# Value projection as seven block products ahead of the heads, and the heads' steps in two queues

## The chip, the cores and the metric

One core of one Trainium2 chip runs the whole layer in one launch. The metric is device time in microseconds, the median of three runs.

## The reference, cut to what matters

One encoder layer on 512 tokens of width 2048, in float32: a token mixer of 8 differential-attention heads and 8 stick-breaking heads, cross-attention into 256 memory tokens, and a SwiGLU feed-forward. Each part has an RMS norm before and after it and a residual. What the change touches:

```python
h = rms_norm(x, g_mix_pre[l])
proj = h @ w_in[l]                      # 2048 x 6144: queries, keys, values of both kinds
a_q, a_k, a_v, b_q, b_k, b_v = jnp.split(proj, ...)
...
out_a = diff_attention(a_q, a_k, a_v, ...)   # 8 heads of 128
out_b = stick_breaking(b_q, b_k, b_v, ...)   # 8 heads of 128
mix = jnp.concatenate([out_a, out_b], axis=-1) @ w_out[l]
```

The values `a_v` and `b_v` together are a product of 512x2048 by 2048x2048.

## The kernel before, in words

**Precision.** Every float32 operand is split in two float32r parts, high and low; a product is three matmuls (high by high, high by low, low by high) that add up in PSUM. A matmul has a 128x128 stationary operand and up to 512 moving columns.

**Weights.** Class `Weights` (L75) goes through a fixed list of chunks of 128x1024 floats (512 KB), in the order in which the kernel uses them. A chunk is loaded by SP's queue into one of `NR` = 5 raw slots, split by ScalarE (L122, a cast) and VectorE (L123, a subtraction) into one of three slots of `parts`, and read by TensorE. `get` (L138) splits two chunks ahead of the one it hands out. For the feed-forward a chunk can be an "add": the raw slot of an earlier chunk stays, and POOL's queue adds another block of the weights to it in flight (L131). Three more raw slots are handed out there by `more` (L94).

**Stages.** The memory stage (`mem_ticks`, L503) projects the memory to keys and values: 64 chunks of 16 matmuls. Beside it the generator `setup_gen` (L416) loads x, takes its norm, and writes the normalised, transposed and split x into the tile `big` (L461 to 469): 16 multiplications (L464) and 16 splits (L231, L232). Then come four groups of four heads (L768): `v_block` (L585) projects the values of a group for all 512 tokens, with 8 chunks of 24 matmuls, and keeps them in SBUF; then each head projects its queries and its keys (`ws_proj`, L540: 48 matmuls each). Then `w_out` (L902), the cross-attention, and the feed-forward, whose products are already done by class `Blocks` (L1184): a product of two by two blocks in seven block products instead of eight, with sums of blocks ahead of it and behind it.

**Side work.** What a head does behind its projections (`diff_gen` L643, `sb_gen` L713, `subnorm` L616) is a generator in the queue `side` (class `Side`, L151): one head at a time. Every six matmuls of a projection call `fill` (L319), which lets `side` go one step, once the number that the step before yielded has been counted down: calls if it is whole, microseconds if it is a float. A step issues some matmuls and the ScalarE and VectorE work on their results; the next step's matmuls read that work. The numbers `YI`, `YS`, `YT`, `SY`, `SZ` and `SL` (L60, L61) are these gaps. The results `mixT` wait in a pool of 50 tiles until `big` is free; the first block of `w_out` runs all of `side` that is left before its last chunk (L907).

**Order.** Beyond the program, a scheduler orders the instructions of each engine; where `pin` (L235) is passed, they stay in program order. An engine runs its instructions in order.

Of the kernel before, what the change touches and what calls it, by code (L numbers as in the profile page):

```python
# [11 lines left out]
F32 = mybir.dt.float32  # L12
# [8 lines left out]
P = 128  # L21
D = 2048
S = 512
# [161 lines left out]

@with_exitstack
def encoder_kernel(ctx: ExitStack, tc: tile.TileContext, a: dict, out: bass.AP):
# [96 lines left out]
    gu_cbs = [(j, NFB + j) for j in range(NFB)]  # L284
    dn_c0 = [2 * sum(DOWN[:b]) for b in range(len(DOWN))]
# [7 lines left out]
    col_pairs = [(0, 1), (2, 3)]  # L293
# [121 lines left out]

    def setup_gen():  # L416
# [34 lines left out]
        def load_xT(kt):  # L451
            if kt < KT:
                xT[kt] = u(s="xT")
                dma(xT[kt], a["xT"][kt])

        for kt in range(3):
            load_xT(kt)
# [43 lines left out]
    unscaled, rbm_done = deque(), []  # L501

    def mem_ticks(name, ct, dst):  # L503
# [18 lines left out]
        while rbm_done and unscaled:  # L522
            t, dst = unscaled.popleft()
            nc.vector.tensor_tensor(t[:, M:512], t[:, 0:M], rbm, op=ALU.mult)
            dma(dst, t[:, M:512])
        fill()
# [13 lines left out]
    def ws_proj(name, ct, lo=0, hi=S):  # L540
        p = ps()
        for half in range(2):
            wh, wl = W.get((name, ct, half))
            wh = wh.rearrange("p (a b) -> p a b", a=8)
            wl = wl.rearrange("p (a b) -> p a b", a=8)
            for k in range(8):
                kt = half * 8 + k
                o, xh, xl = p[:, lo:hi], big[:, 0, kt, lo:hi], big[:, 1, kt, lo:hi]
                mm(o, wh[:, k], xh, start=(kt == 0), stop=False)
                mm(o, wh[:, k], xl, start=False, stop=False)  # L550
                mm(o, wl[:, k], xh, start=False, stop=(kt == KT - 1))
                if k % 2 and kt < KT - 1 and (hi - lo == S or k % 4 == 3):
                    fill()
        return p
# [30 lines left out]
    def v_block(g):  # L585
        accs = [ps() for _ in range(NT)]
        for c in range(8):
            tok_ticks("w_v", g, c, range(NT), accs, from_big, VA <= c < VF)
        r = []
        for t in range(NT):  # L590
            h, l = u(F32R, "vh"), u(F32R, "vl")
            split(h, l, accs[t])
            r.append((h, l))
        fill()
# [21 lines left out]
    def subnorm(o, head, g):  # L616
# [7 lines left out]
        yield 2 if head < KT - 1 else 6.0  # L624
# [142 lines left out]

    for g in range(4):  # L768
        v = v_block(g)
        for h in range(4 * g, 4 * g + 4):  # L770
# [410 lines left out]
    def sub2(o, x, y):  # L1181
        return nc.vector.tensor_tensor(o, x, y, op=ALU.subtract)

    class Blocks:  # L1184

        def __init__(self, name, cbs, c0, n, done, base=None, tile=fu, src=None, every=1,
                     need=None):  # L1190
            self.name, self.cbs, self.c0, self.n, self.done = name, cbs, c0, n, done
            self.base, self.tile, self.src, self.every = base, tile, src or ffn_part, every
            self.T, self.m, self.need = {}, 0, need

        def load_base(self, th, nh):
            if self.base:
                for t in range(2):
                    b = self.T["b", 2 * th + t, nh] = self.tile("base")
                    dma(b, self.base(2 * th + t, nh))

        def product(self, i, apart=False):

            quarter = {1: (0, 0), 5: (0, 1), 3: (1, 1), 6: (1, 0)}.get(i)
            if quarter:
                self.load_base(*quarter)
            p = (ps(), ps())
            ws = []
            for c in range(self.n):
                if self.need:
                    self.need(i, c)  # L1210
                ws.append(W.get((self.name, self.cbs, self.c0 + c, i)))
                if apart:
                    continue
                for k in range(2):
                    for t in range(2):
                        self.mms(p[t], i, c, k, t, ws[c])
            while later:
                later.popleft()()
            for t in range(2):
                if apart:  # L1220
                    for c in range(self.n):
                        for k in range(2):
                            self.mms(p[t], i, c, k, t, ws[c])
                self.evict(i, t, p[t])
                if apart:
                    while later:
                        later.popleft()()

        def mms(self, p, i, c, k, t, w):
            kt = 2 * c + k  # L1230
            wh, wl = (x.rearrange("p (a b) -> p a b", a=2)[:, k] for x in w)
            fh, fl = self.src(i, kt, t)
            mm(p, fh, wh, kt == 0, False)
            mm(p, fh, wl, False, False)
            mm(p, fl, wh, False, kt == 2 * self.n - 1)
            self.m += 1
            if self.m % self.every == 0:
                fill(0.68 * self.every)

        def evict(self, i, t, p):  # L1240

            T = self.T
            add = lambda o, x, y: nc.vector.tensor_tensor(o, x, y, op=ALU.add)
            b = lambda t, nh: T.pop(("b", t, nh))
            if i in (1, 5, 3) or i == 7 and ("r", t) not in T:
                T[i, t] = self.tile(f"p{i}_")
                if i == 3 and self.base:
                    add(T[i, t], p, b(t, 1))
                else:
                    nc.scalar.copy(T[i, t], p)  # L1250
            elif i == 2:
                c = T.pop((1, t)) if ("r", t) in T else self.tile("c11_")
                add(c, p, T.get((1, t), c))
                T["c11", t] = c
                if self.base:
                    later.append(lambda: add(c, c, b(t, 0)))
                later.append(lambda: self.done(t, 0, c))
            elif i == 6:
                r = T.pop((1, t)) if ("c11", t) in T else self.tile("r_")
                sub2(r, p, T.get((1, t), r))  # L1260
# [294 lines left out]
```

## Time and profile before

| what | value |
|---|---|
| median of three runs | 2713.6 us (2713.14 to 2714.34) |
| the profiled execution's own time | 2713.2 us |
| its span, first to last instruction | 2711.4 us |
| TensorE busy | 2665.7 us, 98% |
| VectorE, ScalarE, GpSimd busy | 1636.6, 1294.1, 231.3 us |
| mean granted TensorE clock | 0.996 |
| memory stage, first matmul to last | 7.2 to 194.3 us |
| heads, value blocks included | 194.3 to 842 us |
| output projection starts beside the last heads | 842 us |

Busy time of TensorE is a union of spans whose ends are modelled, since matmuls overlap: the 389 ns that the profile gives for one matmul of 512 columns is its latency, and the spacing of a row of them is read from the time line. Idle time of an engine that nobody waits for costs nothing.

### The profile page before, as it was taken

To read this page: it belongs to the slowest core of one execution; us is meant where nothing else is said; L and a number is where in the kernel's file an instruction comes from. 1 tells how busy PE (TensorE), PEld (TensorE's weight loads), DVE (VectorE), ACT (ScalarE), POOL (GpSimd) and SP (SyncE) were. 2 spreads that over 40 slices of the span, in tenths; PEclk is the share of its full clock that TensorE was granted. 3 is DMA by queue.
4 is the path that set the end of the run, shared out by engine and by line. 5 is a ranking of instruction groups with operands and counts; after the bars stand their busy time and mean duration, and the time that the engine had idled before them with its cause. 6 is when DMAs were issued, how large, how long until landed. Compare 5 with 4: busy or idle time off the path is not lost.

```text
span 2711.4 us, 33630 instructions
## 1 busy us (share of the span) xinstructions
PE 2665.7 (98%) x12704; PEld 2212.9 (82%) x12704; DVE 1636.6 (60%) x2260; ACT 1294.1 (48%) x1892; POOL 231.3 (9%) x273
## 2 busy tenths in 40 slices
PE   8999999999999999999999999999999999999996
PEld 7888777778888789988888888888888888878775
DVE  6672555554445357435567665555556568797887
ACT  5542444445556346334456444444444456454453
POOL 0000000000000000000001212211111121111101
PEclk9999999999999999999999999999999999999998
DMA  8873222222222366223557999888898998788776
GB/s 292 295 266 105 82 86 86 82 82 70 82 80 84 102 212 231 74 98 123 161 173 190 245 256 208 200 204 203 204 209 195 209 223 246 203 263 202 201 204 204
DMA packets 163139, 470.15 MB, mean 173 GB/s; under 512 B 18208, under 2 KB 28856, under 8 KB 162976
## 3 DMA queue, kind: packets, MB, share of 16 engines
q1 hardware_dynamic: 128352, 346.47, 37.7%
q0 software_dynamic: 34624, 121.54, 24.2%
q8 instruction: 99, 1.62, 0.3%
q14 instruction: 64, 0.52, 0.1%
HBM read 431.21 MB, written 39.34 MB: 174 GB/s over the span
## 4 chain that ended last, share of the span: by engine, by line
PE 92%; issue 3%; DVE 2%; DMA 2%; ACT 1%; POOL 1%; SPq 0%; POOLq 0%; ACTq 0%; DVEq 0%
PE ps L228 90%; PE ps L1301 1%; DVE parts L123 1%; DMA xnat<-in_x_dram 1%; PE ps L848 1%; DMA raw<-in_w_dn_dram 0%; ACT parts L122 0%; PE ps L700 0%; POOL y_d L1421 0%; DMA xres<-x_d 0%; DMA raws<-in_w_mk_dram 0%; POOL raws L131 0%; PE ps L982 0%; POOL raw L131 0%; DMA raws<-in_w_dn_dram 0%
## 5 line engine op out<-in xcount | busy, mean ns | idle before, releaser
L228 PE MATMUL ps<-parts,big 128*128 128x512 f32 x4992 | 1168.0, 391 | 10.0 <-ACT parts L122 5.3
L228 PEld LDWEIGHTS ps<-parts,big 128*128 128x128 f32 x4992 | 933.3, 188 | 210.2 <-DVE parts L123 8.0
L123 DVE TENSOR_TENSOR parts<-raws,parts 128x1024 fp32r<-128x1024 f32 x548 | 668.8, 1223 | 596.5 <-ACT parts L122 588.0
L122 ACT CAST parts<-raws 128x1024 fp32r<-128x1024 f32 x548 | 576.3, 1053 | 735.9 <-PE ps L228 666.7
L228 PE MATMUL ps<-parts,form 128*128 128x512 f32 x2376 | 552.4, 390 | 2.3 <-ACT parts L122 2.0
L228 PEld LDWEIGHTS ps<-parts,form 128*128 128x128 f32 x2376 | 444.7, 188 | 96.8 <-ACT parts L122 4.2
L228 PE MATMUL ps<-big,parts 128*128 128x512 f32 x1536 | 375.0, 394 | 0.0
L228 PEld LDWEIGHTS ps<-big,parts 128*128 128x128 f32 x1536 | 282.5, 188 | 61.9 <-issue 4.2
L123 DVE TENSOR_TENSOR parts<-raw,parts 128x1024 fp32r<-128x1024 f32 x178 | 217.0, 1222 | 149.6 <-ACT parts L122 146.1
L122 ACT CAST parts<-raw 128x1024 fp32r<-128x1024 f32 x178 | 187.3, 1054 | 195.7 <-PE ps L228 153.2
L228 PE MATMUL ps<-memhl,parts 128*128 128x512 f32 (+1 forms) x1024 | 183.8, 341 | 8.9 <-DVE memhl L239 7.2
L228 PEld LDWEIGHTS ps<-memhl,parts 128*128 128x128 f32 x1024 | 158.1, 190 | 33.9 <-DVE memhl L239 7.6
L131 POOL DMA_DIRECT2D raws<-in_w_gu_dram x108 | 93.6, 867 | 825.6 <-DVE parts L123 633.4
L380 POOL TENSOR_TENSOR small<-small 128x1 f32<-128x1 f32 (+2 forms) x22 | 16.8, 770 | 1018.9 <-DVE small L379 999.9
L228 PE MATMUL ps<-khl,parts 128*128 128x256 f32 x768 | 96.2, 285 | 0.0
L228 PEld LDWEIGHTS ps<-khl,parts 128*128 128x128 f32 x768 | 93.3, 192 | 0.2
L228 PE MATMUL ps<-big,pTh 128*128 128x512 f32 x256 | 80.2, 392 | 0.0
L228 PE MATMUL ps<-gh,big 128*128 128x512 f32 x256 | 79.2, 389 | 0.0
L131 POOL DMA_DIRECT2D raw<-in_w_gu_dram x60 | 51.9, 866 | 114.0 <-DVE parts L123 114.0
L677 ACT ACTIVATE e<-e,small 128x512 f32<-128x512 f32 (+3 forms) x64 | 35.5, 555 | 53.8 <-DVE small L675 53.8
L228 PEld LDWEIGHTS ps<-gh,big 128*128 128x128 f32 x256 | 48.1, 188 | 9.9
L228 PEld LDWEIGHTS ps<-big,pTh 128*128 128x128 f32 x256 | 47.5, 188 | 9.5
(782 smaller groups left out, 2103.7 us busy)
## 6 DMA issues: line engine op xcount, KB each, us to landing
raws<-in_w_gu_dram POOLq DMA_DIRECT2D x113, 512.0 KB, 6.3
raws<-in_w_gu_dram SPq DMA_DIRECT2D x80, 512.0 KB, 3.8
raws<-in_w_qk_dram SPq DMA_DIRECT2D x64, 512.0 KB, 3.3
raw<-in_w_gu_dram POOLq DMA_DIRECT2D x63, 512.0 KB, 6.2
raw<-in_w_gu_dram SPq DMA_DIRECT2D x60, 512.0 KB, 4.2
aq<-actT_d SPq DMA_DIRECT2D x82, 256.0 KB, 6.2
raws<-in_w_dn_dram SPq DMA_DIRECT2D x41, 512.0 KB, 4.6
raws<-in_w_out_dram SPq DMA_DIRECT2D x40, 512.0 KB, 3.4
```

Source lines behind the costliest of these rows:

```text
L122: self.nc.scalar.copy(h, r)
L123: self.nc.vector.tensor_tensor(l, r, h.bitcast(F32), op=ALU.subtract)
L131: self.nc.gpsimd.dma_start(r, self.chunks[m][3], accum_op=ALU.add)
L228: nc.tensor.matmul(o, l, r, start=start, stop=stop, skip_group_check=True)
L380: nc.gpsimd.tensor_tensor(dst, t, mhalf[:, 0:n], op=ALU.pow)
L677: nc.scalar.activation(es[m][:, 0:n], es[m][:, 0:n], AF.Exp, bias=nmx[:, m : m + 1], accum_out=z[:, m : m + 1],)
L848: nc.tensor.transpose(tp[:, k * P : (k + 1) * P], h[:, k * P : (k + 1) * P], ident)
L1301: nc.tensor.transpose(tp[:, k * P : (k + 1) * P], f[:, k * P : (k + 1) * P], ident)
```

## The change

The value projection moves ahead of all heads and becomes two runs of `Blocks`, one for each half of the columns. A product has 4 chunks and 48 matmuls; 14 products stand in for 32 chunks of 24. That needs the input in eight forms: `in_form` makes four of them in `setup_gen` beside the memory stage (x in quarters of 128x2x256, with three subtractions (L440) and the sum terms for the rest), three at the start of the value stage (`in_forms`), and the last, a plain quarter, when product 5 of the second run has been done. Four of the forms are x's own quarters and lie in `big`, where the heads want them; form 5 lies in the fourth quarter's place until then (`HOMES_IN`). Of each run's chunks, 12 are loaded and 16 are adds on POOL's queue. Three more raw slots serve until the last value chunk. The results go to DRAM (`v_d`) and come back by groups of four heads (`load_v`, `split_v`). The heads go in turn to the queues `side` and `side2`, and `timed` turns whole gaps into microseconds; `fill` is called every three matmuls of a projection, with 0.68. Class `Blocks` itself only moves up in the file.

TensorE's instruction stream at the end of the memory stage (ps_1749, ps_1751), before:

```order
L228 MATMUL ps_1749<-memhl_170,parts 128x512
L228 MATMUL ps_1749<-memhl_170,parts 128x256
L228 MATMUL ps_1793<-parts,big 128x512 x3
L228 MATMUL ps_1794<-parts,big 128x512 x3
L228 MATMUL ps_1795<-parts,big 128x512 x3
L228 MATMUL ps_1796<-parts,big 128x512 x3
```

and now:

```order
L235 MATMUL ps_1751<-memhl_170,parts 128x512
L235 MATMUL ps_1751<-memhl_170,parts 128x256
L235 MATMUL ps_1820<-parts,big 128x512
L235 MATMUL ps_1821<-parts,big 128x512
L235 MATMUL ps_1820<-parts,big 128x512 x2
L235 MATMUL ps_1821<-parts,big 128x512 x2
L235 MATMUL ps_1820<-parts,big 128x512 x3
L235 MATMUL ps_1821<-parts,big 128x512 x3
```

Four PSUM tiles of a value block, one for each 128 tokens, became two tiles of the first block product. The whole stream has 12,730 matmuls before and 12,634 now, 96 fewer, all of the shape 128x512 from `parts`; the counts of every other shape stay.

VectorE's stream in the second half of the memory stage (memev is a memory projection's result, xT and h are input tiles, parts a weight chunk), before:

```order
L123 TENSOR_TENSOR parts<-raws,parts 128x1024
L520 TENSOR_TENSOR memev_1070<-ps_1019,memev_1070 128x256
L232 TENSOR_TENSOR big<-h_79_1047,big 128x512
L232 TENSOR_TENSOR big<-h_83_1089,big 128x512
L524 TENSOR_TENSOR memev_1070<-memev_1070,small 128x256
L123 TENSOR_TENSOR parts<-raws,parts 128x1024
L464 SCALAR_TENSOR_TENSOR h_86_1127<-xT_964,small,rb_1010 128x512
L464 SCALAR_TENSOR_TENSOR h_89_1164<-xT_1045,small,rb_1010 128x512
L123 TENSOR_TENSOR parts<-raws,parts 128x1024
```

and now:

```order
L124 TENSOR_TENSOR parts<-raws,parts 128x1024
L565 TENSOR_TENSOR memev_1171<-ps_1127,memev_1171 128x256
L440 TENSOR_TENSOR xT_964<-xT_964,xT_960 128x512
L494 SCALAR_TENSOR_TENSOR xT_1200<-xT_1200,small,rb_1012 128x256 x2
L494 SCALAR_TENSOR_TENSOR xT_1202<-xT_1202,small,rb_1012 128x256 x2
L124 TENSOR_TENSOR parts<-raws,parts 128x1024
L494 SCALAR_TENSOR_TENSOR xT_1204<-xT_1204,small,rb_1012 128x256 x2
L569 TENSOR_TENSOR memev_1171<-memev_1171,small 128x256
L494 SCALAR_TENSOR_TENSOR xT_1206<-xT_1206,small,rb_1012 128x256
L124 TENSOR_TENSOR parts<-raws,parts 128x1024
```

Between two chunk splits there now stand more operations on x: from the row that spreads the norm (rb) to the last memory result, 29 chunk splits, 29 operations on memory results, 32 multiplications of 256 columns, 16 splits and 16 subtractions of 512 columns.

TensorE's stream where the last head's squares (sqh) are summed; ps_6900 (before) and ps_7019 (now) are the last head's output, before:

```order
L228 MATMUL ps_6900<-wh_6871,vh_5689 128x512
L228 MATMUL ps_6900<-wl_6872,vh_5689 128x512
L228 MATMUL ps_6900<-wh_6871,vl_5690 128x512
L228 MATMUL ps_6927<-sqh_6923,ones_r 128x512
L228 MATMUL ps_6984<-parts,mixh_2460 128x512 x2
L228 MATMUL ps_6984<-parts,mixl_2461 128x512
```

and now, from the row behind the last one of ps_7019:

```order
L235 MATMUL ps_6745<-parts,big 128x512
L235 MATMUL ps_6746<-parts,big 128x512 x3
L235 MATMUL ps_6747<-parts,big 128x512 x3
L235 MATMUL ps_6748<-parts,big 128x512 x3
L235 MATMUL ps_6745<-parts,big 128x512 x3
L235 MATMUL ps_6746<-parts,big 128x512 x3
L235 MATMUL ps_6747<-parts,big 128x512 x3
L235 MATMUL ps_6748<-parts,big 128x512 x3
L235 MATMUL ps_6745<-parts,big 128x512 x3
L235 MATMUL ps_6746<-parts,big 128x512 x3
L235 MATMUL ps_6747<-parts,big 128x512
L235 MATMUL ps_7102<-sqh_7049,ones_r 128x512
```

The sum of squares stood right behind the output that it depends on; now 29 matmuls of the output projection stand between them. Behind the second half of the squares (sql), 43 matmuls stand ahead of the first that reads the last head's result.

The diff, cut to its core:

```diff
+HOMES_IN = {1: (0, 0), 2: (1, 0), 5: (0, 1), 4: (1, 1)}
-YI, YS, YT = 2, (4, 1, 1, 1), (1, 0, 0)
-SY, SZ, SL = 5, 2, 11.0
+YI, YS, YT = 4, (4, 2, 2, 2), (2, 2, 2)
+SY, SZ, SL = 9, 4, 11.0
+TI = 0.5
-VA, VF = 1, 7
...
+def timed(gen):
+    for w in gen:
+        yield (w + TI) * 1.36 if isinstance(w, int) and w else w
...
+    for cbs in col_pairs:
+        wf("w_v", cbs, 0, 4, ORDER, MAKE)
+    n_v = len(chunks)
     for g in range(4):
-        wm("w_v", g, range(8))
         for h in range(4 * g, 4 * g + 4):
             ws("w_qk", qk_cts(h))
...
+    def in_form(i, k2, src, pin=lambda ins: ins):
+        if i in HOMES_IN or i == 0:
+            a_, b_ = HOMES_IN.get(i, HOMES_IN[5])
+            k = 8 * a_ + 2 * k2
+            h, l = (big[:, x, k : k + 2, b_ * M : (b_ + 1) * M] for x in range(2))
+        else:
+            h, l = u2(s="inh"), u2(s="inl")
+        split(h, l, src, pin)
+        infs[i, k2] = (h, l)
...
-        for kt in range(KT):
-            load_xT(kt + 3)
-            t = u(s="h1")
-            nc.vector.scalar_tensor_tensor(
-                t, xT.pop(kt), gains[:, G_MIX + kt : G_MIX + kt + 1], rb,
-                op0=ALU.mult, op1=ALU.mult,
-            )
-            split(big[:, 0, kt], big[:, 1, kt], t)
-            yield 2
+        for k2 in range(4):
+            for n in range(4):
+                a_, th = divmod(n, 2)
+                x = xT[k2, a_, th]
+                for k in range(2):
+                    kt = 2 * (k2 + 4 * a_) + k
+                    nc.vector.scalar_tensor_tensor(
+                        x[:, k], x[:, k], gains[:, G_MIX + kt : G_MIX + kt + 1],
+                        rb[:, th * M : (th + 1) * M], op0=ALU.mult, op1=ALU.mult,
+                    )
+                yield 1
+                i = {(0, 0): 1, (1, 0): 2, (1, 1): 4}.get((a_, th))
+                if i:
+                    in_form(i, k2, x)
+            a11, a21, a12, a22 = (xT.pop((k2, a_, th)) for a_ in range(2) for th in range(2))
+            s = u2(F32, "s7")
+            sub2(s, a21, a11)
+            sub2(a22, a21, a22)
+            yield 1
+            in_form(5, k2, a22)
+            sub2(a11, a11, a22)
+            yield 1
+            sub2(a12, a12, a11)
+            left[k2] = {3: a12, 6: a11, 7: s, 0: a21}
+            for n in range(4):
+                load_xT(4 * k2 + 4 + n)
+            yield 1
...
-    def ws_proj(name, ct, lo=0, hi=S):
+    def ws_proj(name, ct):
...
-                if k % 2 and kt < KT - 1 and (hi - lo == S or k % 4 == 3):
-                    fill()
+                if kt < KT - 1:
+                    fill(0.68)
...
+    def in_forms():
+        for i in (3, 6, 7):
+            for k2 in range(4):
+                in_form(i, k2, left[k2][i], pin)
+                yield 2.0
+        while 5 not in past:
+            yield 0
+        for k2 in range(4):
+            in_form(0, k2, left[k2][0], pin)
+            yield 2.0
...
+    in_raw = [wpool.tile([P, 1024], F32, tag=f"iraw{i}", name=f"iraw{i}") for i in range(NR, NW)]
+    W.more(in_raw, marks[-3], n_v)
+    side.add(in_forms())
+    for n, cbs in enumerate(col_pairs):
+        g = Blocks("w_v", cbs, 0, 4, v_done(cbs), tile=lambda s: u(s=s), src=in_part,
+                   need=in_need)
+        for i in ORDER:
+            g.product(i)
...
-        yield 2 if head < KT - 1 else 6.0
+        yield 9.0
...
+    vr = load_v(0)
     for g in range(4):
-        v = v_block(g)
         for h in range(4 * g, 4 * g + 4):
...
             q = proj_hl("w_qk", cq, scale)
+            if h % 4 == 0:
+                v = split_v(vr)
+            elif h % 4 == 2 and g < 3:
+                vr = load_v(g + 1)
             k = proj_hl("w_qk", ck, 1.0)
-            side.add((diff_gen if h < HD else sb_gen)(h, q, k, v))
+            (side, side2)[h % 2].add(timed((diff_gen if h < HD else sb_gen)(h, q, k, v)))
...
             if cb == 0:
-                if c == 7:
-                    side.drain()
+                while 2 * c + 1 not in mixT:
+                    for s in (side, side2):
+                        if s.q:
+                            s.force()
```

## Rows read from the trace of the kernel before

**Rows 1.** The page's parts 1 and 2: busy time of each engine over the span, and in 40 equal slices TensorE's granted clock.

```profile
span 2711.4 us, 33630 instructions
PE 2665.7 (98%) x12704; PEld 2212.9 (82%) x12704; DVE 1636.6 (60%) x2260; ACT 1294.1 (48%) x1892; POOL 231.3 (9%) x273
...
PEclk9999999999999999999999999999999999999998
```

**Rows 2.** Busy time of each engine by stretch: first the first value block, then the remaining heads' stage, the start of the output projection, most of the gate/up stage, and most of the down stage. Columns: stretch, its length, then busy us (instructions) of PE, PEld, DVE, ACT and POOL, the granted clock, the DMA share and GB/s.

```profile
194.30:237.80 43.50, 43.50 (x194) 35.99 (x193) 11.68 (x12) 10.25 (x12) 0.00 (x0) 1.00 0.42 147
237.80:842.20 604.40, 604.27 (x2883) 488.94 (x2882) 312.29 (x609) 284.31 (x494) 0.00 (x0) 1.00 0.25 83
842.20:907.00 64.80, 60.25 (x282) 48.69 (x281) 29.08 (x37) 31.21 (x52) 0.00 (x0) 1.00 0.24 78
1470.00:2170.00 700.00, 700.00 (x3166) 581.20 (x3166) 408.07 (x422) 331.99 (x375) 131.55 (x152) 1.00 0.90 213
2170.00:2590.00 420.00, 411.59 (x1800) 335.35 (x1799) 331.74 (x388) 217.10 (x269) 59.17 (x68) 0.99 0.84 225
```

**Rows 3.** TensorE in order of time at the first value block: start us, us, engine, line, operation, tiles, shapes, count. The first row is the block, the second the start of the projection behind it.

```profile
194.32 43.75 PE L228 MATMUL ps<-parts,big 128*128 128x512 f32 x192
237.90 24.42 PE L228 MATMUL ps<-big,parts 128*128 128x512 f32 x107
```

**Rows 4.** The same view in the gate/up stage: one product of a block of seven, the first transposes behind it, and the next product.

```profile
1607.38 11.05 PE L228 MATMUL ps<-parts,form 128*128 128x512 f32 x48
1618.27 0.60 PE L1301 MATMUL ps<-small,p__1271_12222 128*128 128x128 f32 x4
1619.06 11.14 PE L228 MATMUL ps<-parts,form 128*128 128x512 f32 x48
```

**Rows 5.** Groups of VectorE instructions: the first five from the stretch 0 to 205 us, the last from the whole span. Columns: line, engine, operation, tiles, shapes, count, busy us, mean ns of one, idle time before them.

```profile
L123 DVE TENSOR_TENSOR parts<-raws,parts 128x1024 fp32r<-128x1024 f32 x68 | 83.0, 1224 | 54.9 <-ACT parts L122 52.4 <-DMA bias_d<-tb_d 1.6 <-DMA raws<-in_w_v_dram 0.8
L520 DVE TENSOR_TENSOR memev<-ps,memev 128x256 f32<-128x256 f32 x32 | 13.4, 417 | 0.0
L464 DVE SCALAR_TENSOR_TENSOR h<-xT,small,rb 128x512 f32<-128x512 f32 x16 | 11.5, 746 | 0.0
L232 DVE TENSOR_TENSOR big<-h,big 128x512 fp32r<-128x512 f32 x16 | 10.5, 683 | 0.0
L239 DVE SCALAR_TENSOR_TENSOR memhl<-memraw,small,memhl 128x256 fp32r<-128x256 f32 x16 | 6.5, 479 | 0.0
...
L1182 DVE TENSOR_TENSOR s<-h,h 128x512 f32<-128x512 f32 x4 | 2.7, 682 | 0.0
```

**Rows 6.** The ScalarE half of a chunk's split, 0 to 205 us, with the same columns.

```profile
L122 ACT CAST parts<-raws 128x1024 fp32r<-128x1024 f32 x68 | 71.3, 1049 | 75.9 <-PE ps L228 65.3 <-ACT big L231 7.7 <-DMA raws<-in_w_mk_dram 2.9
```

**Rows 7.** The memory stage. First, from VectorE in order of time, two chunk splits in a row; then busy time of 10 us while the input is prepared beside the stage, columns as in group 2.

```profile
103.89 1.23 DVE L123 TENSOR_TENSOR parts<-raws,parts 128x1024 fp32r<-128x1024 f32 x1 [1.55 <-ACT parts L122]
106.66 1.23 DVE L123 TENSOR_TENSOR parts<-raws,parts 128x1024 fp32r<-128x1024 f32 x1 [0.76 <-ACT parts L122]
...
150.00:160.00 10.00, 10.00 (x59) 8.82 (x58) 9.14 (x14) 5.26 (x7) 0.00 (x0) 1.00 0.85 286
```

**Rows 8.** TensorE in order of time where the last head ends beside the output projection; in brackets the idle time before a row and what ended it.

```profile
882.66 0.50 PE L228 MATMUL ps<-wh,vh 128*128 128x512 f32 x1 [0.22 <-ACT wh L231]
883.39 0.50 PE L228 MATMUL ps<-wl,vh 128*128 128x512 f32 x1 [0.23 <-DVE wl L232]
886.11 0.50 PE L228 MATMUL ps<-sqh,ones_r 128*128 128x512 f32 x1 [1.99 <-ACT sqh L231]
891.25 0.39 PE L228 MATMUL ps<-sql,ones_r 128*128 128x512 f32 x1
...
898.06 3.01 PE L228 MATMUL ps<-parts,big 128*128 128x512 f32 x12 [0.30 <-ACT big L231]
902.82 9.47 PE L228 MATMUL ps<-parts,big 128*128 128x512 f32 x39 [1.75 <-ACT parts L122]
```

**Rows 9.** VectorE there: the lower half of the split of the last head's result, which the rest of the output block waits for.

```profile
898.67 0.68 DVE L232 TENSOR_TENSOR big<-mixT,big 128x512 fp32r<-128x512 f32 x1
```

**Rows 10.** TensorE in order of time at one stick-breaking head: its last score matmul, the first matmul on the softplus result, and the first of the squares of two heads in a row.

```profile
600.27 0.23 PE L228 MATMUL ps<-mask_b,ident_b 128*128 128x128 bf16 x1
611.09 0.28 PE L228 MATMUL ps<-sph,ntri_r 128*128 128x256 f32 x1
631.87 0.39 PE L228 MATMUL ps<-sqh,ones_r 128*128 128x512 f32 x1
664.83 0.39 PE L228 MATMUL ps<-sqh,ones_r 128*128 128x512 f32 x1
```

**Rows 11.** DMA of 360 us of the gate/up stage: the two queues (packets, MB, share of 16 engines) and the issues of added chunks (count, KB each, median us from issue to landing).

```profile
q0 software_dynamic: 10410, 37.86, 57.5%
q1 hardware_dynamic: 11675, 36.49, 28.7%
raws<-in_w_gu_dram POOLq DMA_DIRECT2D x43, 512.0 KB, 5.7
raw<-in_w_gu_dram POOLq DMA_DIRECT2D x27, 512.0 KB, 5.5
```

**Rows 12.** DMA issues: the input's tiles, 100 to 180 us, and the copies that spread the heads' biases, 150 to 330 us; columns as in group 11.

```profile
xT<-in_xT_dram SPq DMA_DIRECT2D x16, 256.0 KB, 5.0
...
bias_d<-tb_d SPq DMA_DIRECT2D x8, 320.0 KB, 7.0
```

More of the change, by code (lines that the diff above doesn't have):

```diff
@@ L414, in setup_mem, with sub2 @@
         rbm_done.append(True)
+    infs, left = {}, {}
+    def in_form(i, k2, src, pin=lambda ins: ins):
[7 more added lines that the diff above has]
+        infs[i, k2] = (h, l)
+    def sub2(o, x, y):
+        return nc.vector.tensor_tensor(o, x, y, op=ALU.subtract)
     def setup_gen():
@@ L449, in setup_gen, with load_xT @@
         xT = {}
[L451 to L457, printed above, removed]
+        def load_xT(n):
+            if n < 16:
+                k2, a_, th = n // 4, n // 2 % 2, n % 2
+                xT[k2, a_, th] = u2(F32, "xT")
+                dma(xT[k2, a_, th], a["xT"][k2 + 4 * a_, th])
+        for n in range(4):
+            load_xT(n)
         yield 3
@@ new lines, in in_part, with v_done @@
+    def in_part(i, kt, t):
+        return (x[:, kt % 2, t * P : (t + 1) * P] for x in infs[i, kt // 2])
+    def v_done(cbs):
+        return lambda t, nh, c: dma(v_d[cbs[nh], t], c)
+    past = set()
+    def in_forms():
[8 more added lines that the diff above has]
+            yield 2.0
+        left.clear()
@@ new lines, in in_need @@
+    def in_need(i, c):
+        while (i, c) not in infs:
+            side.force()
+    in_raw = [wpool.tile([P, 1024], F32, tag=f"iraw{i}", name=f"iraw{i}") for i in range(NR, NW)]
[6 more added lines that the diff above has]
+            g.product(i)
+            if n:
+                past.add(i)
@@ L589, in v_block, with load_v, split_v @@
+    while later:
+        later.popleft()()
+    side.drain()
+    infs.clear()
+    def load_v(g):
+        vr = [u(s="vr") for _ in range(NT)]
+        for t in range(NT):
+            dma(vr[t], v_d[g, t])
+        return vr
+    def split_v(vr):
         r = []
-        for t in range(NT):
+        for x in vr:
             h, l = u(F32R, "vh"), u(F32R, "vl")
-            split(h, l, accs[t])
+            split(h, l, x, pin)
             r.append((h, l))
-        fill()
         return r
@@ L1178, in encoder_kernel @@
     pT.clear()
[L1181 to L1260, printed above, removed]
-                v, c = T.pop((5, t)), T.pop((3, t))
-                T["r", t], T["v", t] = r, v
-                def sums():
-                    add(v, v, r)
-                    add(c, c, v)
-                later.append(sums)
-                if self.base:
-                    later.append(lambda: add(v, v, b(2 + t, 1)))
-                later.append(lambda: self.done(t, 1, c))
-                if (7, t) in T:
-                    w = T.pop((7, t))
-                    def last():
-                        add(v, v, w)
-                        add(r, r, w)
-                    later.append(last)
-                    later.append(lambda: self.done(2 + t, 1, v))
-            elif i == 7:
-                r, v = T["r", t], T.pop(("v", t))
-                add(v, p, v)
-                add(r, p, r)
-                if self.base:
-                    later.append(lambda: sub2(r, r, b(2 + t, 0)))
-                later.append(lambda: self.done(2 + t, 1, v))
-            elif i == 4:
-                r = T["r", t]
-                sub2(r, p, r)
-                later.append(lambda: self.done(2 + t, 0, r))
@@ L1505, in layout @@
         "x": np.ascontiguousarray(g["x"][0]),
[L1506 removed]
+        "xT": np.ascontiguousarray(
+            g["x"][0].T.reshape(8, 2, P, 2, M).transpose(0, 3, 2, 1, 4)
+        ),
         "mem": np.ascontiguousarray(g["mem"][0]),
```

114 lines of the change are left out of this document (103 added, 11 removed).

## The prediction

> **What bounds the kernel now.** I read the page's busy times first: TensorE is busy 98% of the span at the full clock in all slices [rows 1]. That share alone proves little, since its spans have modelled ends. So I read the stretches that the change touches. In the heads' stage TensorE idles 0.13 us of 604.40, while VectorE works 312.29 us and ScalarE 284.31 us [rows 2]. The reader should see that both have room for half as much again and that nobody waits for them. The value block is one unbroken row [rows 3], and so is a block of seven in the gate/up stage [rows 4], where TensorE has no idle time in 700 us [rows 2]. The only visible waits near the change are at the last head, beside the output projection [rows 2, 8]. So there the time is the number of matmuls times their spacing, and a change pays if it drops matmuls or the few waits at the end, as long as no new wait appears.
>
> The Trainium skill (Perfetto Trace Analysis, "Identifying the Most-Contended Engine") holds matmul busy share to be a poor measure of the distance to the roofline and wants weight-load share and arithmetic instead. Weight loads here are 82% [rows 1], which by that rule leaves TensorE headroom. Taken so, fewer matmuls would buy nothing by themselves, and only terms 2 and 3 below would be left, 2711; by the idle times the matmuls count in full, and the sum goes by these.
>
> **Term 1: fewer matmuls.** 192 matmuls took from 194.32 to 237.90, so 43.58 / 192 = 0.227 us each [rows 3]. Of a block product, 48 took 1607.38 to 1618.27, so 10.89 / 48 = 0.227 too [rows 4]: the moved operand being a weight chunk and the stationary one the input costs the same either way. I do not take the rows' own spans, which overlap. 32 chunks of 24 are 768 matmuls; 14 products of 48 are 672. The 96 that go are worth 96 x 0.2266 = **21.75 us**. The counts of all other shapes stay, so nothing is given back on TensorE itself.
>
> **Term 2: the last head.** Before, TensorE idles there 0.22 and 0.23 us for the last weights of the head, 1.99 for the squares, and 0.30 and 1.75 at the remaining chunk, 4.49 us in sum [rows 8] (4.55 by the stretch, 64.80 - 60.25 [rows 2]). The chain that it waited for is the same work now. But 29 matmuls (6.6 us) stand between the head's output and the squares, which took 883.39 + 0.50 to 886.11, 2.2 us. 43 matmuls (9.7 us) cover the rest, which took from 891.25 [rows 8] to 898.67 + 0.68 [rows 9], 8.1 us. So 1.99 and 0.30 should go, and the small ones with two heads interleaved; the 1.75 is a wait for a chunk's split on a crowded ScalarE and can stay. I take **-3**, between -4.5 (all goes) and 0 (the last two heads, now finishing together, wait for each other).
>
> **Term 3: the memory stage.** Here VectorE has the least room. A chunk's split comes every 106.66 - 103.89 = 2.77 us, and in a crowded 10 us VectorE works 9.14 while TensorE idles 0.00 [rows 7]. To the sums in the changed order: 29 chunk splits of 1.22 us, 29 operations on memory results of 0.42, 32 multiplications of 256 columns of 0.48 (a row with two inputs, a scalar and 256 columns), 16 splits of 0.68 and 16 subtractions of 0.68 [rows 5]: 35.5 + 12.1 + 15.3 + 10.9 + 10.9 = 84.7 us. That work now has 30 chunks, 30 x 2.77 = 83 us. The rows' durations overlap: in the crowded stretch successive VectorE instructions start some 0.09 us before the end of the one ahead. The 122 instructions thus need about 77.5 us back to back: 93%. Filled, but not over. What delays TensorE is not the mean but the longest pile ahead of one split: rb's copy (0.68) and up to four multiplications, 2 us or so late. A chunk is split two ahead, 5.54 us, of which the two halves take 1.05 [rows 6] and 1.22 us; 3.3 us are left. So no wait, with little to spare. I add **+1** for an unlucky pile; the ends are 0 and +14 (first rival).
>
> **Term 4: the value stage.** Its chunk is 12 matmuls, 2.72 us, the cadence of the gate/up stage, where VectorE, ScalarE and POOL were busy 58%, 47% and 19% and TensorE never waited [rows 2]. The adds come as densely as there: 43 + 27 in 360 us are one in 5.1 us [rows 11], here 32 in 152 us are one in 4.75. Here there is less beside it (no activations), plus 12 splits of input forms in the run-up, of 0.68 us on VectorE: 8 us in 150. DMA per run of 7 products (76 us): 12 loads of 512 KB are 6.29 MB, 8 results 2.1 MB, 16 adds 8.39 MB. The gate/up stage moved 36.49 MB by the hardware queue in 28.7% of 360 us, 2.83 us a MB, and 37.86 by the software queue in 57.5%, 5.47 us a MB [rows 11]. That makes 8.39 x 2.83 + 8.39 x 5.47 = 70 us, 91% (gate/up 90% [rows 2]). An add lands after 5.7 us [rows 11], and the raw slots let it be issued up to ten chunks, 27 us, ahead. I take **0**; fed like the down stage, which idles 8.41 us of 420 [rows 2], 152 us would lose 3.
>
> **Hidden, at 0.** Results to DRAM and back are 16 stores and 16 loads of 256 KB, of which a like load lands after 5.0 us [rows 12]; group 0 is read back behind a first query projection of 48 matmuls, 10.9 us. The new order splits values beside the key projection: 8 splits per group that ScalarE and VectorE did before too. Evictions and sums go where VectorE is 58% busy. Without value blocks the heads' stage is 604 - 131 = 473 us with some 280 us of VectorE work, 60%. The gap from a head's scores to its next matmuls was 600.27 to 611.09, 10.8 us of a head's 33 [rows 10]; the new numbers in time give about the same, with a second head between, so more matmuls cover it.
>
> **Sum.** The profiled execution took 2713.2 us, 0.4 below the median of the three runs. 2713.2 - 21.75 - 3 + 1 = 2689.4; on the median, **2690**. The forecast's own range is 2684 to 2697: the last head's ends (-1.5, +3), the memory stage, and 3 us of the down stage's kind.
>
> **Rivals.**
> *The input comes late.* The x tiles now live until a whole group of four is finished, and the next four loads are issued only then; each lands 5.0 us later [rows 12]. If the multiplications wait for it, VectorE's queue, which is in order, holds the next chunk's split behind them, and TensorE waits: four times 5.0 less the 1.55 us that VectorE can stand idle ahead of a split [rows 7], 14 us. Time 2690 + 14 = 2704. For it: VectorE at 93%. Against: the buffers may hold a second group. Chance 0.12.
>
> *The value stage is bound by the DMA.* The heads' biases are spread in its first run, 8 copies of 320 KB [rows 12], 2.62 MB and another 7.4 us of the hardware queue: 77.6 us of transfers for 76 us of matmuls. If the lead does not carry that, TensorE waits up to those 7.4 us there and 1.5 (the down stage's 2%) in the second run: 2690 + 9 = 2699. For it: the copies took 7.0 us to land, the slowest of all [rows 12]. Against: before, they fell into the same stretch without a wait, though at a DMA share of 0.42 [rows 2]. Chance 0.07. The Trainium skill (SBUF — State Buffer, the trap of "DVE blocks DMA" and "Who interferes with whom") adds a reason for it: descriptors of a DMA issued by POOL starve while VectorE runs a two-port operation. [...]
>
> *Slower: two heads wait for each other.* The steps of both queues share one order on ScalarE and VectorE. A step of one head that stands behind a long piece of the other makes TensorE's next step wait, and everything behind it. An uncovered head cost 0.22 + 0.23 + 1.99 = 2.44 us [rows 8]. If every one of 16 heads paid that, 39 us: 2713.2 - 21.75 + 39 = 2730. It decides from ten heads on (24 us). For it: the stick-breaking heads use ScalarE for most of their time. Against: 0.13 us idle in 604 [rows 2] with one queue, and time-based gaps no shorter. Chance 0.07.
>
> *The saved matmuls buy nothing.* Then something else than TensorE sets the cadence of the value blocks: 2713.6 - 3 + 1, 2711 or 2712. Against: no idle time ahead of a matmul in 43.5 us, and one spacing in two places that differ in everything else [rows 3, 4]. Chance 0.02.
>
> **Chances.** Forecast 0.72, the first rival 0.12, the DMA 0.07, the heads 0.07, nothing saved 0.02. The range must leave out no more than 2 in 10, so it takes the forecast's own 2684 to 2697 and goes on over the DMA's 2699 to the first rival, 2704; the heads alone, and tails of the others, are left out. 0.2% is 5.4 us, about what a measurement of this kernel can tell from no change. Faster by more: forecast, first rival and DMA, 0.91, less 0.03 for two of them at once or a milder form of the heads' wait, which end within 0.2%: 0.88, 0.05 and, by the heads, slower 0.07.
>
> **What would show it.** Right: the value stage, 14 products, lasts 152 us from about 194 with no TensorE idle time; the heads' stage about 473 us with less than 1 us idle; the 4.5 us at the last head shrink to 2 or less; the memory stage still ends near 194. Wrong: TensorE waits for parts between 110 and 194 us (first rival; the row behind it names xT); waits for parts in the value stage whose raws land late (second); waits for the softplus results, the weights or the squares of a head, spread over all heads (third).

## The result, and the profile after

The changed kernel takes **2678.65 us** (median of 4 runs, 2676.92 to 2680.80) against 2713.37: a ratio of 0.9872, interval 0.9855 to 0.9889, or 34.7 us less. The forecast was 2690 us, 23.4 us less than before, with a range of 2684 to 2704. The sign and the largest term were right; the gain is half as large again, and the time lies below the range.

The page's first parts, answering to [rows 1]:

```profile
span 2676.3 us, 33793 instructions
PE 2636.4 (99%) x12608; PEld 2193.3 (82%) x12608; DVE 1702.5 (64%) x2363; ACT 1329.8 (50%) x1944; POOL 257.6 (10%) x305
...
PEclk9999999999999999999999999999999999999998
```

Busy time by stretch, columns as in [rows 2]: the value stage, the heads until the output projection starts, and the last heads beside it.

```profile
193.20:345.50 152.30, 152.30 (x674) 126.12 (x673) 94.01 (x102) 74.00 (x85) 26.62 (x31) 1.00 0.94 236
345.50:804.10 458.60, 458.60 (x2258) 370.43 (x2258) 277.48 (x578) 251.30 (x465) 0.00 (x0) 1.00 0.27 88
804.10:880.00 75.90, 75.82 (x356) 62.95 (x355) 38.49 (x49) 37.51 (x60) 0.00 (x0) 1.00 0.27 85
```

TensorE has no idle time in 152.30 and in 458.60 us. The heads' stage was forecast at 473 us; it is shorter mainly because the output projection now starts earlier among the heads' matmuls, so that 2258 of them stand in it where 2883 less three value blocks of 192 would be 2307. The forecast and the gain are therefore compared below between marks that both kernels share.

TensorE in order of time at the last product of the value stage and the first projection behind it:

```profile
334.66 11.04 PE L235 MATMUL ps<-parts,big 128*128 128x512 f32 x48
345.54 6.74 PE L235 MATMUL ps<-big,parts 128*128 128x512 f32 x29
```

A product lasts 10.88 us, as [rows 4] has it, and the stage 345.54 - 193.20 = 152.34 us, where four value blocks took 4 x 43.58 = 174.3 [rows 3]: 22.0 us less.

The last head, in order of time, where [rows 8] shows five waits:

```profile
848.00 0.39 PE L235 MATMUL ps<-wh,vl 128*128 128x512 f32 x1
848.22 6.74 PE L235 MATMUL ps<-parts,big 128*128 128x512 f32 x29
854.79 0.39 PE L235 MATMUL ps<-sqh,ones_r 128*128 128x512 f32 x1
855.02 0.61 PE L235 MATMUL ps<-parts,big 128*128 128x512 f32 x2
855.48 0.39 PE L235 MATMUL ps<-sql,ones_r 128*128 128x512 f32 x1
...
863.86 39.35 PE L235 MATMUL ps<-parts,big 128*128 128x512 f32 x171
```

No row has an idle time in brackets. 171 matmuls from 863.86 run through the place where the kernel before waited for the last result and for a chunk.

The crowded 10 us of the memory stage, answering to [rows 7], and DMA issues of the value stage, answering to [rows 11, 12]:

```profile
150.00:160.00 10.00, 10.00 (x59) 8.71 (x58) 10.00 (x19) 6.09 (x9) 0.00 (x0) 1.00 0.78 263
160.00:170.00 10.00, 10.00 (x59) 8.73 (x59) 9.45 (x15) 4.29 (x6) 0.00 (x0) 1.00 0.93 320
```

```profile
raws<-in_w_v_dram POOLq DMA_DIRECT2D x19, 512.0 KB, 9.4
iraw<-in_w_v_dram POOLq DMA_DIRECT2D x12, 512.0 KB, 8.9
...
bias_d<-tb_d SPq DMA_DIRECT2D x8, 320.0 KB, 11.2
```

VectorE is full for 10 us and TensorE does not notice. The adds land after some 9 us instead of 5.7 and the bias copies after 11.2 instead of 7.0, at a DMA share of 0.94: the second rival's contention is there, and TensorE has no idle time from it. Why the adds land later, no run separates; that the lead of the raw slots is what absorbs it is the prediction's argument and was not tested.

**Where the time went.** I cut each trace at two marks that both kernels have: the first matmul on value weights, and the first transpose of the sum behind the output projection. Ahead of the first mark the time is 194.3 us before and 193.2 after; between them 815.5 and 783.8; behind the second, to the last matmul, 1679.2 and 1677.1. So 31.75 of 35.0 us lie between the marks. The matmuls are 21.75 of them. About 10 are left, where the last head's waits were forecast at 3.

Within these 10 us, the last head's waits are 5.8: before, its gaps exceed the spacing by 6.2 us (the 4.5 of [rows 8] and the slower start of the matmuls behind each wait), after by 0.35. The next piece is in rows that no wait marks. A differential head's scores come as two halves of three 64-row matmuls. A run of such matmuls between two others is called a score stretch below. In the trace of before, one stretch with both halves, and one place where the scheduler had put a projection matmul between them:

```profile
311.10 0.84 PE L228 MATMUL ps<-big,parts 128*128 128x512 f32 x3
311.88 0.39 PE L228 MATMUL ps<-ph,ph 64*128 64x256 f32 x2
312.10 0.29 PE L228 MATMUL ps<-pl,ph 64*128 64x256 f32 x2
312.21 0.28 PE L228 MATMUL ps<-ph,pl 64*128 64x256 f32 x2
312.43 3.06 PE L228 MATMUL ps<-big,parts 128*128 128x512 f32 x12
315.42 0.38 PE L228 MATMUL ps<-ph,ph 64*128 64x256 f32 x1
315.64 0.28 PE L228 MATMUL ps<-pl,ph 64*128 64x256 f32 x1
315.75 0.27 PE L228 MATMUL ps<-ph,pl 64*128 64x256 f32 x1
315.96 0.50 PE L228 MATMUL ps<-big,parts 128*128 128x512 f32 x1
316.39 0.38 PE L228 MATMUL ps<-ph,ph 64*128 64x256 f32 x1
316.61 0.28 PE L228 MATMUL ps<-pl,ph 64*128 64x256 f32 x1
316.73 0.27 PE L228 MATMUL ps<-ph,pl 64*128 64x256 f32 x1
```

Six matmuls take 311.88 to 312.43, 0.55 us; three alone take 315.42 to 315.96, 0.54. The halves run side by side when they stand together, and one after the other when they don't. Counted from the start of the matmul ahead to the start of the one behind, less 0.227, all score stretches sum to 28.2 us before (37 of them) and 25.4 after (33): 2.85 us. The Trainium skill (TensorEngine Tiling (Array Packing), "Key Properties") says that tiles of the array work independently, and that a change of the tiling mode drains the engine. The rows agree with the first, 0.55 us for both halves against 0.54 for one. No row shows a drain; that a stretch has a fixed cost, as the second would give it, is measured below with two score steps at once.

### The profile page after: what moved, and what is told of

It reads as the page before. It is cut to its first block, busy times and chain, and to the rows that moved or that the text cites. A ratio compares the mean times of both kernels' runs of the same rounds, so it can differ in the third digit from the quotient of the medians.

```text
span 2676.3 us, 33793 instructions
## 1 busy us (share of the span) xinstructions
PE 2636.4 (99%) x12608; PEld 2193.3 (82%) x12608; DVE 1702.5 (64%) x2363; ACT 1329.8 (50%) x1944; POOL 257.6 (10%) x305
## 4 chain that ended last, share of the span: by engine, by line
PE 87%; issue 5%; DMA 4%; DVE 3%; POOL 1%; ACT 0%; SPq 0%; POOLq 0%; ACTq 0%; DVEq 0%
PE ps L235 85%; DMA aq<-actT_d 1%; DVE parts L124 1%; DMA xres<-x_d 1%; PE ps L1396 1%; DMA xnat<-in_x_dram 1%; DMA raws<-in_w_dn_dram 1%; PE ps L1053 1%; DMA raw<-in_w_dn_dram 0%; POOL y_d L1516 0%; PE ps L901 0%; ACT parts L123 0%; POOL raws L132 0%; DVE aq L1438 0%; DMA y_d<-p__1733_18500 0%
## 5 line engine op out<-in xcount | busy, mean ns | idle before, releaser
L235 PE MATMUL ps<-parts,big 128*128 128x512 f32 x4608 | 1070.5, 390 | 7.4 <-DVE parts L124 3.2
L235 PEld LDWEIGHTS ps<-parts,big 128*128 128x128 f32 x4608 | 862.1, 188 | 190.5 <-DVE parts L124 7.5
L235 PE MATMUL ps<-big,parts 128*128 128x512 f32 x1536 | 380.5, 395 | 0.0
L235 PE MATMUL ps<-parts,inh 128*128 128x512 f32 x192 | 59.1, 389 | 0.0
```

The costliest lines, as they stand in the source:

```text
L235: nc.tensor.matmul(o, l, r, start=start, stop=stop, skip_group_check=True)
```

## The experiments

Times are medians; ratios are to the kernel before, run beside them on the same chip.

**One queue, first try.** The heads back in one queue, shorter gaps.

```diff
-YI, YS, YT = 4, (4, 2, 2, 2), (2, 2, 2)
-SY, SZ, SL = 9, 4, 11.0
+YI, YS, YT = 3, (5, 2, 2, 2), (2, 1, 1)
+SY, SZ, SL = 14, 5, 11.0
...
-        yield 9.0
+        yield 3 if head < KT - 1 else 6.0
...
-            (side, side2)[h % 2].add(timed((diff_gen if h < HD else sb_gen)(h, q, k, v)))
+            side.add((diff_gen if h < HD else sb_gen)(h, q, k, v))
```

> The changed kernel with its heads back in one queue: gaps counted in calls again, shortened so that a head fits into its 32 calls (score gaps 3 and 5,2,2,2, then 2,1,1; softplus 14, 5; 3 before the squares). The value projection stays as changed. Theory (the change gained 21.75 us by matmuls, about 6 at the last head's waits and about 3 because the 64-row score matmuls of a differential head's two halves stand together more often): the last head is uncovered again, +6 to the 2678.7 of the changed kernel, and in this order the score matmuls stand in 48 separate stretches instead of 33, 15 more at 0.65 us, +10: 2694 us. Rival (separated score matmuls cost nothing, only waits do): +6, 2685 us. Second rival (one queue can't cover a head's chain now that a head has 29 us instead of 36): idle time of TensorE at every head, 1 us or more each, 2700 or above.

Measured: 2783.3 us, 1.0256 (1.0242 to 1.0270). The second rival, and far beyond its 2700. The list of waits of TensorE from 350 to 1010 us (what it waited for, us in total, times, longest; sqh are the squares, pp a differential head's probabilities, ptl and pth these transposed and split, sph a stick-breaking head's softplus, wh and wl its weights):

```profile
PE ps L235 <- ACT sqh L238: 29.9, 15, 2.0
PE ps L901 <- DVE pp L888: 11.4, 5, 2.3
PE ps L235 <- DVE ptl L239: 5.9, 7, 1.3
```

Fifteen of the 16 heads wait for their squares. From 350 to 950 us the granted clock is 0.93 to 0.95 in every 100 us, where the heads of the kernel before have 1.00; the waits at the last head of that kernel did not lower it. Windows of this run at its first head's squares, columns as in [rows 2]:

```profile
396.00:400.00 4.00, 1.14 (x4) 0.52 (x4) 1.25 (x3) 2.10 (x4) 0.00 (x0) 1.00 0.37 131
400.00:402.00 2.00, 2.00 (x8) 1.65 (x8) 1.05 (x2) 0.22 (x1) 0.00 (x0) 0.82 0.00 0
402.00:404.00 2.00, 2.00 (x6) 1.52 (x5) 0.00 (x0) 0.00 (x0) 0.00 (x0) 0.50 0.00 0
404.00:406.00 2.00, 2.00 (x8) 1.59 (x8) 0.00 (x0) 0.00 (x0) 0.00 (x0) 0.82 0.00 0
406.00:408.00 2.00, 2.00 (x9) 0.88 (x8) 0.00 (x0) 0.66 (x1) 0.00 (x0) 1.00 0.00 0
```

0.50 is the lower of the two levels, 1.2 GHz. The gaps were mine and could have been at fault, so the theory of the score matmuls can't be read from this run; the queue was tried again with the gaps of the kernel before.

**One queue, gaps of before in microseconds.**

```diff
-YI, YS, YT = 4, (4, 2, 2, 2), (2, 2, 2)
-SY, SZ, SL = 9, 4, 11.0
+YI, YS, YT = 2, (4, 1, 1, 1), (1, 0, 0)
+SY, SZ, SL = 5, 2, 11.0
...
-        yield 9.0
+        yield 2 if head < KT - 1 else 6.0
...
-            (side, side2)[h % 2].add(timed((diff_gen if h < HD else sb_gen)(h, q, k, v)))
+            side.add(timed((diff_gen if h < HD else sb_gen)(h, q, k, v)))
```

> The changed kernel with its heads in one queue, but with the gaps that the kernel before had, in microseconds (2; 4,1,1,1; 1,0,0; 5, 2; 2 before the squares, 6 us for the last head), a side step possible every three matmuls. It asks whether the value projection needs the second queue. Theory (a single queue covers a head's chain as it did before, and only the last head and the score matmuls lose): +5.8 us at the last head, and 37 stretches of score matmuls with ten lone halves, +4.5 us: 2689 us. Rival (with 29 us a head instead of 36 one queue runs late, and steps are taken without cover): idle time of TensorE at most heads, 3 to 6 us each as in the one-queue run before, 2710 us or more.

Measured: 2793.7 us, 1.0297 (1.0282 to 1.0313): the rival again. TensorE's waits from 194 to 1100 us:

```profile
PE ps L901 <- DVE pp L888: 20.7, 8, 5.8
PE ps L235 <- ACT sqh L238: 18.0, 9, 2.0
PE ps L235 <- ACT sph L238: 15.4, 7, 3.7
```

The squares of the first and the last head in this run, and of the first head in the changed kernel (its last head's are shown above) and in the kernel before (its last in [rows 8]):

```profile
406.38 0.39 PE L235 MATMUL ps<-sqh,ones_r 128*128 128x512 f32 x1
968.77 0.39 PE L235 MATMUL ps<-sqh,ones_r 128*128 128x512 f32 x1
```

```profile
421.54 0.39 PE L235 MATMUL ps<-sqh,ones_r 128*128 128x512 f32 x1
```

```profile
299.74 0.39 PE L228 MATMUL ps<-sqh,ones_r 128*128 128x512 f32 x1
```

968.77 - 406.38 over 15 heads is 37.5 us a head (37.0 in the first try, with other gaps); in the changed kernel, 854.79 - 421.54, it is 28.9. In these two tries with one queue a head takes some 37 us. Before, the matmuls of a head and its share of a value block took (886.11 - 299.74) / 15 = 39.1 us (not the 36 of the expectations), and no head but the last made TensorE wait. With the values moved ahead, 29 us of matmuls are left, and TensorE waits at most heads. Shown are the waits and the three paces; the 37 us hold waits and a lowered clock, so how long a head's chain is by itself was not measured, and neither was one queue with other gaps.

**Two queues alone.** The kernel before with the heads' part of the change; value blocks stay.

```diff
-YI, YS, YT = 2, (4, 1, 1, 1), (1, 0, 0)
-SY, SZ, SL = 5, 2, 11.0
+YI, YS, YT = 4, (4, 2, 2, 2), (2, 2, 2)
+SY, SZ, SL = 9, 4, 11.0
+TI = 0.5
...
+        yield (w + TI) * 1.36 if isinstance(w, int) and w else w
...
-                if k % 2 and kt < KT - 1 and (hi - lo == S or k % 4 == 3):
-                    fill()
+                if kt < KT - 1:
+                    fill(0.68)
...
-        yield 2 if head < KT - 1 else 6.0
+        yield 9.0
...
-            side.add((diff_gen if h < HD else sb_gen)(h, q, k, v))
+            (side, side2)[h % 2].add(timed((diff_gen if h < HD else sb_gen)(h, q, k, v)))
...
-                if c == 7:
-                    side.drain()
+                while 2 * c + 1 not in mixT:
+                    for s in (side, side2):
+                        if s.q:
+                            s.force()
```

> The kernel before, with only the heads' part of the change: two queues, gaps in microseconds, a side step possible every three matmuls; value blocks stay as they were. Theory: the matmul count stays, the last head's waits go (-5.8 with their after-effects), and the 64-row score matmuls stand in 32 stretches instead of 37 or 38 (-3.3): 2713.4 - 9 = 2704 us, with no idle time of TensorE inside the heads' stage. Rival (the two queues gain only what waits showed): 2707 or 2708. Rival of the prediction (two heads wait for each other): above 2715.

Measured: 2702.2 us, 0.9956 (0.9942 to 0.9969). The theory's 2704 lies at the upper end of the interval (2697 to 2704), the rival's 2707 outside. Between the marks it has 805.0 us, 10.5 less than before, and no wait. Busy time of the heads' stage and at the last heads, columns as in [rows 2]:

```profile
193.10:828.00 634.90, 634.90 (x3039) 517.10 (x3038) 321.73 (x616) 290.62 (x501) 0.00 (x0) 1.00 0.26 87
828.00:900.00 72.00, 72.00 (x339) 60.16 (x338) 34.33 (x43) 35.29 (x58) 0.00 (x0) 1.00 0.27 88
```

Its score stretches sum to 24.95 us (32 of them), 3.3 less. With the 6.2 at the last head that is 9.5 of the 10.5. The changed kernel stands another 21.2 us below this one between the marks, though it has 0.4 more in score stretches and 0.35 of gaps: the value products alone are worth 22.0 us here, against a term of 21.75.

**Score matmuls kept together in the kernel before.** TensorE in program order through the heads' stage, and nothing else.

```diff
-        nc.tensor.matmul(o, l, r, start=start, stop=stop, skip_group_check=True)
+        i = nc.tensor.matmul(o, l, r, start=start, stop=stop, skip_group_check=True)
+        if pinned:
+            pin(i)
...
+    pinned.append(1)
     for g in range(4):
...
+    pinned.clear()
```

> The kernel before, with nothing changed but that TensorE's instructions stay in program order through the heads' stage, so that the two halves' score matmuls of a differential head are never separated: 32 stretches instead of 38. Theory: -2.9 to -3.3 us, 2710 us, the last head's waits as before. Rival (separation costs nothing): 2713.4 or more, as the order has less freedom.

Measured: 2708.4 us, 0.9983 (0.9975 to 0.9992), 4.5 us less, interval 2.2 to 6.8. Between the marks 811.1, 4.4 less; the score stretches sum to 24.8 us, so 3.4 of it is theirs. The other 1.0 us is at the last head: its three long waits are as before, but the two short ones for its weights, 0.22 and 0.23 us, are gone, and its gaps exceed the spacing by 5.2 us instead of 6.2. So the theory holds for the 3.4 us: a gain that no wait and no dropped matmul explains.

**The same edit in the changed kernel.**

> The changed kernel, TensorE in program order through the heads' stage: 32 stretches of score matmuls instead of 33. Theory: -0.5 us, which a timing can't tell; the trace shows no stretch of 2 or 4 matmuls. If the scheduler's freedom covers waits, they appear here as idle time ahead of the softplus, weight or square matmuls, up to 2 us a head: 2680 to 2710.

Measured: 2684.05 us, 0.9889 (0.9875 to 0.9902). The score stretches are 32, but the scheduler's freedom was worth more. TensorE's one wait, and the stretch behind it with columns as in [rows 2]:

```profile
PE ps L235 <- ACT pth L242: 3.5, 1, 3.5
```

```profile
617.00:620.00 3.00, 2.88 (x7) 2.18 (x8) 1.75 (x4) 0.73 (x2) 0.00 (x0) 0.50 0.00 0
```

This wait, where the differential heads end, and the lower clock behind it are what the trace shows for the 5.5 us that this kernel takes more than the changed one between the marks.

**Two score steps at once.** To price a score stretch by itself, on the changed kernel; TensorE stays in program order through the differential heads.

```diff
+            if i:
+                sc = scores(i)
+            else:
+                sc = sc0
+            if i == 1:
+                sc0 = scores(0)
...
+    pinned.append(1)
     vr = load_v(0)
...
+            if h == 8:
+                pinned.clear()
```

> The changed kernel with the last two score steps of a differential head issued together, and TensorE in program order while the differential heads run: 24 stretches of 64-row matmuls instead of 33, eight of them with 12 matmuls. Theory (a stretch costs 0.29 us besides its matmuls, whatever their number: 645 ns for six of 256 columns, where 3 x 117 ns are 351 for both halves side by side): the stretches' sum falls from 25.4 to 22.5 us, so 2675.8 us if nothing else waits. Rival (12 matmuls cost twice what 6 cost): 25 us again, 2678.7. In program order a weight or softplus wait of some 4 us can come where the differential heads end, as in the pinned run.

Measured: 2682.0 us, 0.9885 (0.9868 to 0.9901). A merged stretch, in order of time:

```profile
384.26 0.39 PE L235 MATMUL ps<-ph,ph 64*128 64x256 f32 x2
384.49 0.29 PE L235 MATMUL ps<-pl,ph 64*128 64x256 f32 x2
384.60 0.29 PE L235 MATMUL ps<-ph,pl 64*128 64x256 f32 x2
384.72 0.28 PE L235 MATMUL ps<-ph,ph 64*128 64x256 f32 x2
384.84 0.29 PE L235 MATMUL ps<-pl,ph 64*128 64x256 f32 x2
384.96 0.28 PE L235 MATMUL ps<-ph,pl 64*128 64x256 f32 x2
385.17 9.86 PE L235 MATMUL ps<-big,parts 128*128 128x512 f32 x42
```

Twelve take 0.91 us where twice six take 1.1. By the same count as above a merged stretch is 1.00 us against 2 x 0.645, and all 24 sum to 22.7 us, as forecast to 0.2. The time did not follow: the order now brings 5.0 us of waits, among them 1.9 for the squares of head 7 and, at the last head, 0.3 for its result and 1.8 for a chunk. Between the marks it takes 786.2 us, 2.4 more than the changed kernel; 2.7 saved and 5.0 waited come to 2.3.

**The same with 11 us ahead of the squares**, where the changed kernel yields 9.

> As the run with two score steps at once, but 11 us instead of 9 before the squares; in its order at least 5.5 us of matmuls stand ahead of every head's squares, where that run had 0.9 us at head 7 and 1.6 at the last. Theory: the 24 stretches of score matmuls stay (22.7 us instead of 25.4), and the waits of that run, 4.6 us at the last head and at head 8 together, go: 2.7 us below the changed kernel beside it, some 2676. Rival (program order makes a new wait wherever it is moved to): 2679 or more, with idle time named in the list of waits.

Measured: 2679.6 us, 0.9872 (0.9856 to 0.9889): the rival. The stretches sum to 22.4 us, and the waits are elsewhere:

```profile
PE ps L235 <- ACT parts L123: 1.6, 1, 1.6
PE ps L235 <- DVE wl L243: 0.9, 1, 0.9
PE ps L235 <- ACT wh L242: 0.6, 1, 0.6
```

Between the marks it takes 785.4 us, 1.6 more than the changed kernel: 3.0 saved, 3.1 waited, and a granted clock of 0.98 from 700 to 800 us. So no version here beats the changed kernel, and the times of the two can't be told apart.

**The changed kernel again.**

> The changed kernel once more, beside the run above, to see what two traces of the same kernel differ by: 2678.7 us; from the first value matmul to the first transpose of the residual 783.8 us within 1, behind that 1677 within 5, as other kernels with the same code there had 1675.7 to 1683.6.

Measured: 2679.3 us, 0.9870 (0.9855 to 0.9885). Between the marks 783.74 us, against 783.76: in these two traces, where TensorE never waits there, that part of the time repeats to hundredths. Behind the second mark it is 1676.5. Over all ten traces, whose code behind the second mark is the same, that part is 1675.7 to 1683.6; and the first mark lies at 192.2 to 194.3 us, with the old memory stage and the new alike.

## Why the prediction missed its range

- **Term 1**, -21.75: right in size, 22.0 measured between the two kernels with two queues. The sentence that closed it is the step that failed: "The counts of all other shapes stay, so nothing is given back on TensorE itself." The counts stay, but the time of 64-row matmuls depends on what stands beside them, and the new order moved them: -2.85 us, a term that the sum put at nothing; keeping the score matmuls together in the kernel before, with the value blocks as they were, gained 3.4. The rows of the order were at hand, and so was the place at 315 us in the trace of before; I compared counts and shapes, not neighbours.
- **Term 2**, -3: right in kind, mis-sized; it measured -5.8, beyond its own end of -4.5. The 1.75 us for a chunk went too, which I had left standing. And a wait costs more than its idle time, since the matmuls behind it start slower: 6.2 against 4.5 us.
- These two bring the forecast from 2690 to some 2684, the edge of the range. The rest of the miss is smaller pieces that the sum did not hold: the +1 of term 3, 1.1 us ahead of the first mark, 2.1 us behind the second, and about 1 us of the 31.75 between the marks that is not attributed.
- **Term 3**, +1: 0. VectorE was full in the crowded 10 us, and TensorE did not idle there. The working has a slip: 122 instructions that overlap by 0.09 us need 84.7 - 11.0 = 73.7 us and not 77.5, so 89% and not 93. The 1.1 us by which the first mark moved is inside the scatter of ten traces.
- **Term 4**, 0: right; the products lasted 152.3 us. The adds landed at 9 us, not at 5.7, without effect.
- The 2.1 us behind the second mark lie inside the scatter of the traces, 1675.7 to 1683.6. The medians leave a doubt: the difference of medians, less what lies between the marks, is 3.0 and 3.2 us for the two measurements of the changed kernel (0.2 to 4.5 over all seven runs with the values ahead), and 0.1 us for each of the two that keep the value blocks. Whether a part of it belongs to the change stays open.
- **The rival with two queues** had its sign the wrong way round. With two queues no head made TensorE wait (0.00 us idle in 458.60); with one, in both tries, most heads did, once the value blocks were gone. I read 0.13 us of idle time as room, while the runs speak for cover, that is, work that TensorE could do while a head's chain ran on ScalarE and VectorE. And the rival's price, 2.44 us a head, was too low: the second one-queue run takes 115 us more than the changed kernel between the marks, 7 for each of 16 heads, with waits for pp (20.7 us) and the softplus (15.4) besides the squares (18.0) and a granted clock of 0.91 to 0.97 from 350 to 950 us. The two parts of the change are no sum: values first with one queue is 70 and 79 us slower than before in the two tries, two queues alone are 11 faster, both 35 faster.

## What to carry to other kernels

No idle time on the bounding engine doesn't say how much cover there is; measure the length of one dependent chain against the work that runs beside it, before that work is taken away. When the order of a bound engine changes, compare neighbours and not counts alone: the 64-row matmuls here cost by stretch and not by number. And cut repeated traces at common marks: here the part between them repeated to hundredths in two traces, while the rest scattered by a few microseconds.

## What was not expected of the hardware

- Two halves of three 64-row matmuls of 256 columns take 0.55 us together and 0.54 each alone; a score stretch costs about 0.29 us beyond its 256-column matmuls at 0.117, whether these are six or twelve (0.645 and 1.00 us).
- After waits of 0.88 and 1.99 us close together (TensorE busy 1.14 of 4 us) the granted clock went to 0.50, the lower of its two levels, and was back at 1.00 from 406 us, 6 us behind the second wait; at the last head of the kernel before, waits of 0.22, 0.23 and 1.99 us (TensorE busy 1.68 of 4 us) left it at 1.00.
